# Eight pieces in one operation in the first FFN group, and matmul operands moved to multiples of 512 bytes

## The chip, the core and the metric

The kernel runs on one core of one Trainium2 chip. The metric is the device time of one execution in microseconds (us). The kernel before takes 2956.35 us, the median of three runs from 2955.74 to 2959.2 us.

## The reference

One layer of a streaming encoder is computed for 64 new frames of a running stream ("sample"), 16 meta tokens and 2048 frames of a new stream ("prompt"): 2128 rows of width 1024. The rows go through a projection into three head groups (differential attention, RG-LRU, gated linear attention), an output projection, and an FFN with a causal convolution of width 3 along the rows, separately for the two streams:

```
hn = rms_norm(x, prm['norm_ffn_g'][l])
u = hn @ prm['ffn_w_up'][l]
uc, ffn_c1 = causal_dwconv(u, ffn_c0, prm['ffn_conv_w'][l], prm['ffn_conv_b'][l])
x = x + (jax.nn.gelu(uc) * (hn @ prm['ffn_w_gate'][l])) @ prm['ffn_w_down'][l]
```

The FFN width is 2816. The convolution needs the two rows before each row: zeros ahead of the prompt's first row, two rows of state ahead of the sample's first.

## The kernel before, in words

Activations lie transposed: features on the 128 partitions, rows along the free dimension. Every product is taken with three matmuls of split operands (high by high, high by low, low by high), whose elements have 4 bytes. A weight tile of 128 by 1024 (`whi`, `wlo`, three buffers each) holds eight slices of 128 columns; each matmul loads one slice as its weights and streams a second operand of up to 512 columns past it.

The work of TensorE (PE) is one long stream, `dense`: the input projection (`win`, matmuls at L641 and L643), then the FFN three times, for the row groups `FGROUPS = [[512], [512], [336, 256, 512]]`. Attention (`ps_sc`, `ps_pt`, `ps_o`) and the recurrences are woven into the first part of it by a scheduler that sets each engine's order when the program is built; the third group runs alone. Within a group `wout` (L1434) makes the output projection, its norm fills `h2h`/`h2l`, `up_gate` makes for each of 22 tiles of 128 FFN features the products `pu` and `pg` (L1299) and their activation into `gh`/`gl`, and `down` (L1366) multiplies four such tiles at a time with the down weights into `pd`.

In `up_gate` of the first group the 512 rows are two pieces, the 64 sample rows ("s") and 448 rows of the prompt ("z"). For each piece every step is issued by itself: ACT copies `pu` behind two columns of history in `uh` (L1316) and makes the first tap `cc` (L1321), DVE adds two taps (L1323), ACT squares (L1326), DVE (L1327), ACT takes tanh (L1329); after `pg` two DVE operations (L1334, L1336), POOL rounds into `gh` (L154) and DVE takes the rest `gl` (L157). `uh` and `cc` have two buffers each (`ev2`), so the two pieces of one feature tile fill both.

Where the tiles lie, as the built program has it (bytes within a partition): `whi` begins at 16928, `wlo` at 29216, 32 bytes past a multiple of 512, and so do all their slices. `h2h` and `gh` of the first two groups begin at 41504 and 90656, 32 past a multiple too, with slices 2048 bytes apart. In the third group `h2h`/`h2l` of the 256 and 512 rows are 480 bytes past a multiple (`h2h` of the 512 rows at 196576), and its `gh`/`gl`, 1104 columns long, lie 4416 bytes apart, so that their parts begin at many distances from one. The 256-column operands of `win` are 32 past. The order of allocation gives these places; no engine waits on them.

Of the kernel before, what the change touches and what calls it, by code (L numbers as in the profile page):

```python
# [135 lines left out]
def tile_hymba_step(ctx, tc, xT, xkT, cache_v, wi, wo, wu, wg, wd, par, sgla, c_msk, yT_p, yT_s, nkT_p, nv_p, lh_p, lc_p, gs_p, fc_p,  # L136
# [1138 lines left out]

    def up_gate(g, ff, H, gt, norms):
        (wu_,), (wg_,) = w_take(("up", g, ff), 1), w_take(("gate", g, ff), 1)
        ev2, gp = env["ev"], env["gp"]
        gw = sum(FGROUPS[g])
# [5 lines left out]
        goff = 0  # L1285
        for bi, n in enumerate(FGROUPS[g]):
            yield from norms.pop(bi, ())
            us = []
            for a, b, kind in ffn_pieces(g, n):
                uh = ev2.tile([P, n + 2], F32, tag="uh", name="uh")  # L1290
                cc = ev2.tile([P, n], F32, tag="cc", name="cc")
                us.append((a, b, kind, uh, cc))
# [38 lines left out]
            pg = env["prod"]
            for a, b, kind, uh, cc in us:
                m = b - a
                nc.vector.scalar_tensor_tensor(out=cc[:, :m], in0=cc[:, :m], scalar=0.5, in1=pg[:, a:b], op0=ALU.mult,  # L1334
                                               op1=ALU.mult)
                nc.vector.scalar_tensor_tensor(out=cc[:, :m], in0=uh[:, :m], scalar=1.0, in1=cc[:, :m], op0=ALU.add,  # L1336
                                               op1=ALU.mult)
                gh_, gl_ = gh[:, goff + a:goff + b], gl[:, goff + a:goff + b]
                pool_scaled(gh_, cc[:, :m])
# [295 lines left out]
```

## Time and profile before

| | before |
|---|---|
| median of three runs | 2956.35 us |
| profiled execution | 2957.12 us, span 2955.3 us (1.8 us lie around the span) |
| PE busy | 2841.2 us, 96% of the span |
| DVE, ACT, POOL busy | 1890.9, 1138.1, 870.5 us |
| mean granted TensorE clock | 0.98 of full speed |
| input projection | 0 to 817 us |
| FFN group 1, 2, 3 | 817 to 1487, to 2022, to 2955.3 us |

Times in the text are microseconds from the span's start. A matmul's own duration in the profile includes its way through the array and overlaps its neighbours; what a matmul costs in a dense run is the distance from its start to the next start. The stages are told apart by where `wout` (L1434) begins.

### The profile page before, as it was taken

To read this page: it belongs to the slowest core of one execution; us is meant where nothing else is said; L and a number is where in the kernel's file an instruction comes from. 1 tells how busy PE (TensorE), PEld (TensorE's weight loads), DVE (VectorE), ACT (ScalarE), POOL (GpSimd) and SP (SyncE) were. 2 spreads that over 40 slices of the span, in tenths; PEclk is the share of its full clock that TensorE was granted. 3 is DMA by queue.
4 is the path that set the end of the run, shared out by engine and by line. 5 is a ranking of instruction groups with operands and counts; after the bars stand their busy time and mean duration, and the time that the engine had idled before them with its cause. 6 is when DMAs were issued, how large, how long until landed. Compare 5 with 4: busy or idle time off the path is not lost.

```text
span 2955.3 us, 44538 instructions
## 1 busy us (share of the span) xinstructions
PE 2841.2 (96%) x16031; PEld 2508.7 (85%) x16031; DVE 1890.9 (64%) x3699; ACT 1138.1 (39%) x2589; POOL 870.5 (29%) x1212
## 2 busy tenths in 40 slices
PE   7999999999898998999999999999999999999997
PEld 7988899989876887787787888888989998999997
DVE  7677685778879879879969865333454333333335
ACT  5354554555555454545445433211222121212122
POOL 4435534434535445444424221000110000000001
PEclk9999999999999999999999999999999999999999
DMA  7675564656796776777875565685222222222222
GB/s 241 201 217 148 179 214 139 199 179 186 227 338 212 252 264 234 249 266 261 285 258 183 197 203 183 208 327 186 72 86 86 86 86 86 86 86 86 86 86 105
DMA packets 277930, 537.43 MB, mean 182 GB/s; under 512 B 31014, under 2 KB 170030, under 8 KB 277710
## 3 DMA queue, kind: packets, MB, share of 16 engines
q1 hardware_dynamic: 277566, 534.58, 54.9%
q8 instruction: 127, 2.08, 0.3%
q14 instruction: 93, 0.76, 0.1%
q10 hardware_dynamic: 144, 0.01, 0.0%
HBM read 382.74 MB, written 151.76 MB: 181 GB/s over the span
## 4 chain that ended last, share of the span: by engine, by line
PE 69%; DVE 14%; DMA 4%; issue 2%; ACT 2%; POOL 1%; SPq 0%; POOLq 0%; ACTq 0%; DVEq 0%
PE pd L1366 15%; PE pg L1299 14%; PE pu L1299 14%; PE pd L1434 6%; PE ps_w L641 5%; PE ps_w L643 3%; DVE pc L1100 3%; PE ps_o L1166 3%; PE ps_sc L1059 2%; PE ps_pt L1151 2%; PE ps_sc L1052 2%; DVE BD L886 1%; DVE NB L1061 1%; PE ps_r L891 1%; DVE y L435 1%
## 5 line engine op out<-in xcount | busy, mean ns | idle before, releaser
L257 POOL TENSOR_TENSOR wlo<-raw,whi 128x1024 fp32r<-128x1024 f32 (+1 forms) x104 | 249.8, 2404 | 309.6 <-ACT whi L151 278.5
L1062 ACT ACTIVATE pc<-ps_sc,NB 128x512 f32<-128x512 f32 (+6 forms) x400 | 224.5, 562 | 298.2 <-DVE NB L1061 262.6
L1299 PE MATMUL pu<-h2h,whi 128*128 128x512 f32 (+2 forms) x880 | 316.8, 360 | 5.0 <-ACT h2h L151 2.8
L1323 DVE SCALAR_TENSOR_TENSOR cc<-uh,prm,cc 128x512 f32<-128x512 f32 (+4 forms) x264 | 165.0, 634 | 242.9 <-ACT cc L1321 239.8
L1299 PE MATMUL pu<-h2l,whi 128*128 128x512 f32 (+2 forms) x880 | 316.2, 359 | 1.4 <-DVE h2l L157 1.4
L1299 PE MATMUL pu<-h2h,wlo 128*128 128x512 f32 (+2 forms) x880 | 316.5, 360 | 0.0
L1366 PE MATMUL pd<-gh,whi 128*128 128x512 f32 (+2 forms) x880 | 314.2, 360 | 2.1 <-DMA whi<-WS 1.4
L1299 PE MATMUL pg<-h2h,wlo 128*128 128x512 f32 (+2 forms) x880 | 315.6, 359 | 0.4 <-DMA wlo<-WS 0.4
L1299 PE MATMUL pg<-h2l,whi 128*128 128x512 f32 (+2 forms) x880 | 315.9, 359 | 0.0
L1299 PE MATMUL pg<-h2h,whi 128*128 128x512 f32 (+2 forms) x880 | 315.0, 358 | 0.7 <-DMA whi<-WS 0.5
L1366 PE MATMUL pd<-gh,wlo 128*128 128x512 f32 (+2 forms) x880 | 314.5, 358 | 0.0
L1366 PE MATMUL pd<-gl,whi 128*128 128x512 f32 (+2 forms) x880 | 312.9, 357 | 0.0
L1372 DVE TENSOR_TENSOR x<-x,pd 128x512 f32<-128x512 f32 (+2 forms) x240 | 141.8, 595 | 217.1 <-PE pd L1366 216.1
L641 PE MATMUL ps_w<-hh,whi 128*128 128x384 f32 (+2 forms) x768 | 259.1, 340 | 16.0 <-ACT whi L151 10.5
L1316 ACT ACTIVATE uh<-pu 128x336 f32<-128x336 f32 (+3 forms) x132 | 59.3, 464 | 539.6 <-PE pu L1299 539.1
L1061 DVE TENSOR_REDUCE NB<-ps_sc 128x1 f32<-128x512 f32 (+6 forms) x400 | 209.5, 529 | 86.8 <-PE ps_sc L1059 85.2
L641 PE MATMUL ps_w<-hl,whi 128*128 128x384 f32 (+2 forms) x768 | 259.6, 339 | 0.4 <-DVE hl L157 0.4
L641 PE MATMUL ps_w<-hh,wlo 128*128 128x384 f32 (+2 forms) x768 | 256.0, 335 | 0.3 <-DVE wlo L157 0.3
L154 POOL TENSOR_SCALAR gh<-cc 128x336 fp32r<-128x336 f32 (+3 forms) x132 | 72.9, 553 | 444.8 <-DVE cc L1336 440.0
L151 ACT ACTIVATE whi<-raw 128x1024 fp32r<-128x1024 f32 (+2 forms) x160 | 165.8, 1036 | 96.7 <-DMA raw<-in_wi 30.5
L1299 PEld LDWEIGHTS pu<-h2h,whi 128*128 128x128 f32 x880 | 167.4, 190 | 26.6 <-ACT h2h L151 3.2
L154 POOL TENSOR_SCALAR pc<-pc,fr 128x512 f32<-128x512 f32 (+4 forms) x200 | 156.8, 802 | 109.3 <-DVE fr L1082 86.1
(330 smaller groups left out, 7142.5 us busy)
## 6 DMA issues: line engine op xcount, KB each, us to landing
whi<-WS SPq DMA_DIRECT2D x148, 512.0 KB, 4.3
wlo<-WS SPq DMA_DIRECT2D x148, 512.0 KB, 4.3
raw<-in_wi SPq DMA_DIRECT2D x74, 512.0 KB, 4.1
WS<-whi SPq DMA_DIRECT2D x74, 512.0 KB, 3.1
WS<-wlo SPq DMA_DIRECT2D x74, 512.0 KB, 6.0
Kc<-KHL SPq DMA_DIRECT2D x48, 512.0 KB, 5.8
V<-VHL SPq DMA_DIRECT2D x48, 512.0 KB, 3.5
Q<-QHL SPq DMA_DIRECT2D x64, 256.0 KB, 4.4
```

The source lines that it names most:

```text
L151: nc.scalar.activation(out=out, in_=in_, func=AF.Copy, scale=scale)
L154: nc.gpsimd.tensor_scalar(out, in_, s, 1.0, ALU.mult, ALU.mult)
L257: nc.gpsimd.tensor_tensor(out=lo[:, :n], in0=t[:, :n], in1=f(hi[:, :n]), op=ALU.subtract)
L641: nc.tensor.matmul(ps[:, :n], lhsT=wx, rhs=hx, start=st_, stop=sp_)
L643: nc.tensor.matmul(ps[:n, :wd_], lhsT=hx, rhs=wx, start=st_, stop=sp_)
L1061: nc.vector.tensor_reduce(NB[:qw, ti, m, ci:ci + 1], ps[:qw, :kt_], AX.X, ALU.min)
L1062: nc.scalar.activation(out=pv_[m][:qw, :kt_], in_=ps[:qw, :kt_], func=AF.Exp, scale=-1.0, bias=NB[:qw, ti, m, ci:ci + 1], accum_out=SS[:qw ...
L1299: nc.tensor.matmul(ps[:, :n], lhsT=w_[wi_][:, k * P:(k + 1) * P], rhs=hx, start=(k == 0 and i3 == 0), stop=(k == KT - 1 and i3 == 2))
L1323: nc.vector.scalar_tensor_tensor(out=cc[:, :m], in0=uh[:, w:w + m], scalar=cw[w], in1=cc[:, :m], op0=ALU.mult, op1=ALU.add)
L1366: nc.tensor.matmul(ps[:, :n], lhsT=w_, rhs=g_[:, o:o + n], start=(j == 0 and i3 == 0), stop=(j == len(gts) - 1 and i3 == 2))
L1372: nc.vector.tensor_tensor(x2[b, ct], x2[b, ct], ps[:, :n], ALU.add)
L1434: nc.tensor.matmul(ps[:, :n], lhsT=w_, rhs=g_, start=(k == 0 and i3 == 0), stop=(k == KT - 1 and i3 == 2))
```

## The change

In the first group the 512 rows of a feature tile are now eight pieces of 64 columns. `uh` has room for eight times 66 columns, and each step is issued once over all eight: the copy of `pu` writes 8 by 64 columns, a small ACT operation fills the two history columns of pieces 2 to 7 from the end of the piece before (read from `pu`), and POOL fills those of piece 0 (state) and piece 1 (zeros) as it did. `uh` and `cc` are one tile each per feature tile now, in the same two buffers. The other groups take the same code with one piece.

A tile of 480 bytes, set once by POOL, stands ahead of the weights; a second of 480 bytes ahead of the third group's right-hand pools and a third of 64 bytes ahead of its `gh`. In the third group `gh`/`gl` hold the 512 rows first, then 336 (in room for 384), then 256. In the built program `whi` now begins at 17408, `h2h` of the first two groups at 41984, `gh` at 91136, `h2h` of the third group's 512 rows at 196096 and its `gh` at 83456 with 4608 bytes between tiles, all multiples of 512. (The slices of the 336 rows' `h2h` are 1344 bytes apart, so only the first of them lies on one.)

```
+    nc.gpsimd.memset(cst.tile([P, 120], F32, name="pad0"), 0.0)
...
+        pad(p2.enter_context(tc.tile_pool(name="pad_r", bufs=1, side="right")), 480)
...
+        pad(p2.enter_context(tc.tile_pool(name="pad_l", bufs=1)), 64)
...
-            for a, b, kind, uh, cc in us:
-                m = b - a
...
-                nc.scalar.activation(out=uh[:, 2:2 + m], in_=pu[:, a:b], func=AF.Copy)
...
-                nc.scalar.activation(out=cc[:, :m], in_=uh[:, 0:m], func=AF.Identity, scale=cw[0], bias=cb)
...
+            pu = env["prod"][:, :n].rearrange("p (c t) -> p c t", t=t)
+            nc.scalar.activation(out=uh[:, :, 2:], in_=pu, func=AF.Copy)
+            if g == 0:
+
+                nc.gpsimd.tensor_copy(uh[:, 0, 0:2], pr("fst", 0, 44).rearrange("p (w k) -> p k w", w=2)[:, ff, :])
+                nc.gpsimd.memset(uh[:, 1, 0:2], 0.0)
+                nc.scalar.activation(out=uh[:, 2:, 0:2], in_=pu[:, 1:n // t - 1, t - 2:], func=AF.Copy)
+                nc.gpsimd.tensor_copy(fce[:, 1, :, ff], uh[:, 0, t:])
...
+            nc.scalar.activation(out=cc, in_=uh[:, :, 0:t], func=AF.Identity, scale=cw[0], bias=cb)
+            for w in (1, 2):
+                nc.vector.scalar_tensor_tensor(out=cc, in0=uh[:, :, w:w + t], scalar=cw[w], in1=cc, op0=ALU.mult,
+                                               op1=ALU.add)
...
+    def places(g):
+
+        at, n = {}, 0
+        for b in sorted(range(len(FGROUPS[g])), key=lambda b: -FGROUPS[g][b]):
+            at[b] = n
+            n += -(-FGROUPS[g][b] // P) * P
+        return at, n
+
+    def pad(pool, n):
+        nc.gpsimd.memset(pool.tile([P, n // 4], F32, tag="pad", name="pad", bufs=1), 0.0)
```

ACT's order around one feature tile of the first group, before (`whi<-raw` splits weights, `pc,SS<-ps_sc` is attention's exponential, `ph<-ps_pt` rounds its weights):

```order
L1316 ACTIVATE uh<-pu 128x64
L1316 ACTIVATE uh<-pu 128x448
L1321 ACTIVATE cc<-uh,prm 128x64
L1062 ACTIVATE pc,SS<-ps_sc,NB 128x16
L151 ACTIVATE ph<-ps_pt 128x512
```

```order
L1321 ACTIVATE cc<-uh,prm 128x448
L1326 ACTIVATE uh<-cc 128x64
L1329 ACTIVATE uh<-uh 128x64
L1326 ACTIVATE uh<-cc 128x448
L1329 ACTIVATE uh<-uh 128x448
```

Between the two stands one more row of attention; the second piece follows the first at each step. The same feature tile now:

```order
L1312 ACTIVATE uh<-pu 128x8x64
L1317 ACTIVATE uh<-pu 128x6x2
L1322 ACTIVATE cc<-uh,prm 128x512
L1063 ACTIVATE pc,SS<-ps_sc,NB 128x16
L151 ACTIVATE ph<-ps_pt 128x512
```

```order
L1328 ACTIVATE uh<-cc 128x8x64
L1330 ACTIVATE uh<-uh 128x8x64
L151 ACTIVATE whi<-raw 128x1024
L1063 ACTIVATE pc,SS<-ps_sc,NB 128x144 x2
L151 ACTIVATE oo<-oSs 128x256
```

Eight operations of the convolution became five, and the attention rows between them kept their places. On DVE, a place a little later in the first group, before (`att`, `EK`, `BD` are the gated linear attention, `pl` is attention's):

```order
L1327 SCALAR_TENSOR_TENSOR uh<-uh,cc 128x64
L1323 SCALAR_TENSOR_TENSOR cc<-uh,prm,cc 128x448
L895 COPY_PREDICATED att<-msk,ps_r 128x64x4
L157 TENSOR_TENSOR pl<-ps_pt,ph 16x256
L1327 SCALAR_TENSOR_TENSOR uh<-uh,cc 128x448
L1334 SCALAR_TENSOR_TENSOR cc<-cc,pg 128x64
L1334 SCALAR_TENSOR_TENSOR cc<-cc,pg 128x448
L1336 SCALAR_TENSOR_TENSOR cc<-uh,cc 128x64
L1336 SCALAR_TENSOR_TENSOR cc<-uh,cc 128x448
```

and the same steps now:

```order
L1329 SCALAR_TENSOR_TENSOR uh<-uh,cc 128x8x64
L896 COPY_PREDICATED att<-msk,ps_r 128x64x4
L879 TENSOR_TENSOR EK<-bl 128x128
L880 TENSOR_TENSOR EK<-bl 128x128
L157 TENSOR_TENSOR pl<-ps_pt,ph 16x256
L1333 SCALAR_TENSOR_TENSOR cc<-cc,pg 128x512
L1334 SCALAR_TENSOR_TENSOR cc<-uh,cc 128x512
```

The 64-column operations are gone and two rows of the recurrence moved in among the rest. On PE no matmul is added or removed; in the first group attention's matmuls stand a few places earlier or later among those of the FFN, and ahead of it and in the third group the order is the same.

## Rows read from the trace of the kernel before

**Rows 1.** The page: busy time and share of the span of each engine, and the chain that ended last by engine.

```profile
PE 2841.2 (96%) x16031; PEld 2508.7 (85%) x16031; DVE 1890.9 (64%) x3699; ACT 1138.1 (39%) x2589; POOL 870.5 (29%) x1212
...
PE 69%; DVE 14%; DMA 4%; issue 2%; ACT 2%; POOL 1%; SPq 0%; POOLq 0%; ACTq 0%; DVEq 0%
```

**Rows 2.** Busy time of each engine by stage (input projection, FFN groups 1, 2 and 3), then the mean granted clock, the DMA engines' busy share and GB/s.

```profile
0.00:817.00 817.00, 763.40 (x4928) 719.50 (x4929) 611.35 (x1287) 414.76 (x1022) 358.29 (x403) 0.97 0.65 195
817.00:1487.00 670.00, 635.66 (x3120) 521.13 (x3119) 577.76 (x1128) 348.69 (x808) 306.19 (x384) 0.97 0.77 260
1487.00:2022.00 535.00, 528.57 (x2581) 438.98 (x2580) 321.57 (x587) 182.79 (x407) 113.76 (x192) 0.99 0.66 225
2022.00:2955.30 933.30, 913.59 (x5407) 829.08 (x5405) 380.19 (x700) 191.89 (x356) 92.21 (x233) 0.99 0.25 90
```

**Rows 3.** Group 1 (817 to 1487): whom PE and ACT waited for, total us, times, longest us; then the chain by line in the same stretch.

```profile
PE ps_sc L1052 <- ACT pc L1062: 16.3, 15, 3.5
...
ACT pc L1062 <- DVE NB L1061: 112.4, 66, 8.1
...
ACT cc L1321 <- DVE gl L157: 9.8, 3, 5.9
```

```profile
by line: PE pd L1366 11.6%; PE pu L1299 7.4%; DVE pc L1100 7.1%; PE pg L1299 6.8%; PE pd L1434 6.6%; issue 5.1%; PE ps_o L1166 4.2%; DVE BD L886 3.4%; DVE NB L1061 3.4%; DVE cc L1323 3.2%; PE ps_sc L1059 2.9%; PE ps_sc L1052 2.9%; PE ps_pt 
```

**Rows 4.** The convolution's DVE operations in group 1 by shape: count, busy us and mean ns of one, idle before.

```profile
L1323 DVE SCALAR_TENSOR_TENSOR cc<-uh,prm,cc 128x448 f32<-128x448 f32 x44 | 33.8, 768 | 1.4 <-ACT cc L1321 1.2
L1323 DVE SCALAR_TENSOR_TENSOR cc<-uh,prm,cc 128x64 f32<-128x64 f32 x44 | 20.6, 468 | 6.2 <-ACT cc L1321 6.0
L1336 DVE SCALAR_TENSOR_TENSOR cc<-uh,cc 128x448 f32<-128x448 f32 x22 | 15.7, 714 | 0.2
L1327 DVE SCALAR_TENSOR_TENSOR uh<-uh,cc 128x448 f32<-128x448 f32 x22 | 15.1, 688 | 2.2 <-ACT uh L1326 2.1
L157 DVE TENSOR_TENSOR gl<-cc,gh 128x448 fp32r<-128x448 f32 x22 | 13.6, 618 | 2.2 <-POOL uh L1313 1.7 <-POOL gh L154 0.2
L1334 DVE SCALAR_TENSOR_TENSOR cc<-cc,pg 128x448 f32<-128x448 f32 x22 | 13.5, 612 | 0.0
L1336 DVE SCALAR_TENSOR_TENSOR cc<-uh,cc 128x64 f32<-128x64 f32 x22 | 10.7, 488 | 0.1
L157 DVE TENSOR_TENSOR gl<-cc,gh 128x64 fp32r<-128x64 f32 x22 | 5.6, 253 | 0.3
L1327 DVE SCALAR_TENSOR_TENSOR uh<-uh,cc 128x64 f32<-128x64 f32 x22 | 4.7, 214 | 0.7 <-ACT uh L1326 0.7
L1334 DVE SCALAR_TENSOR_TENSOR cc<-cc,pg 128x64 f32<-128x64 f32 x22 | 4.7, 212 | 0.5 <-PE pg L1299 0.3
```

**Rows 5.** The same operations with 512 columns, over the whole span.

```profile
L1323 DVE SCALAR_TENSOR_TENSOR cc<-uh,prm,cc 128x512 f32<-128x512 f32 x88 | 66.6, 758 | 148.2 <-ACT cc L1321 146.9
...
L1336 DVE SCALAR_TENSOR_TENSOR cc<-uh,cc 128x512 f32<-128x512 f32 x44 | 30.8, 699 | 3.4
...
L157 DVE TENSOR_TENSOR gl<-cc,gh 128x512 fp32r<-128x512 f32 x44 | 30.4, 692 | 27.1 <-POOL gh L154 26.4 <-POOL r L414 0.7
L1327 DVE SCALAR_TENSOR_TENSOR uh<-uh,cc 128x512 f32<-128x512 f32 x44 | 30.4, 691 | 26.6 <-ACT uh L1326 26.4
L1334 DVE SCALAR_TENSOR_TENSOR cc<-cc,pg 128x512 f32<-128x512 f32 x44 | 30.2, 686 | 33.3 <-PE pg L1299 33.1
```

**Rows 6.** A run of 512-column matmuls of group 2 without a break, weights and streamed operand 32 bytes past a multiple of 512: first and 49th start (start us, duration us).

```profile
1905.10 0.39 PE L1299 MATMUL pu<-h2h,wlo 128*128 128x512 f32 x1
...
1915.98 0.39 PE L1299 MATMUL pu<-h2h,wlo 128*128 128x512 f32 x1
```

**Rows 7.** The same in group 3, streamed operand 480 past: 512 columns, first and 48th; 256 columns, first and 48th.

```profile
2414.32 0.40 PE L1299 MATMUL pu<-h2h,whi 128*128 128x512 f32 x1
...
2425.29 0.40 PE L1299 MATMUL pg<-h2h,wlo 128*128 128x512 f32 x1
```

```profile
2408.67 0.28 PE L1299 MATMUL pu<-h2h,whi 128*128 128x256 f32 x1
...
2414.20 0.28 PE L1299 MATMUL pg<-h2h,wlo 128*128 128x256 f32 x1
```

**Rows 8.** `down` of group 3, one run of 512 columns, first and 12th; and 256-column matmuls of the input projection, both operands 32 past, first and 27th.

```profile
2331.32 0.39 PE L1366 MATMUL pd<-gh,whi 128*128 128x512 f32 x1
...
2333.85 0.39 PE L1366 MATMUL pd<-gl,whi 128*128 128x512 f32 x1
```

```profile
397.21 0.28 PE L643 MATMUL ps_w<-whi,hl 128*128 128x256 f32 x1
...
400.31 0.28 PE L643 MATMUL ps_w<-whi,hh 128*128 128x256 f32 x1
```

**Rows 9.** The two runs' stretches: busy PE, PEld, DVE, ACT, POOL, then clock, DMA share, GB/s.

```profile
1905.00:1916.00 11.00, 11.00 (x51) 9.10 (x50) 3.59 (x6) 2.68 (x4) 1.26 (x5) 1.00 0.95 346
2414.30:2425.50 11.20, 11.20 (x50) 9.06 (x49) 3.90 (x7) 3.18 (x6) 0.72 (x3) 1.00 0.25 94
```

**Rows 10.** From the page, matmuls by line over the span (each of L1299 in six such rows, L1366 and L641 in three).

```profile
L1299 PE MATMUL pu<-h2h,whi 128*128 128x512 f32 (+2 forms) x880 | 316.8, 360 | 5.0 <-ACT h2h L151 2.8
...
L1366 PE MATMUL pd<-gh,whi 128*128 128x512 f32 (+2 forms) x880 | 314.2, 360 | 2.1 <-DMA whi<-WS 1.4
...
L641 PE MATMUL ps_w<-hh,whi 128*128 128x384 f32 (+2 forms) x768 | 259.1, 340 | 16.0 <-ACT whi L151 10.5
```

**Rows 11.** What POOL's pacing copies of group 3's loads (L1392) waited for, total us and times; and a fill of 128 columns at the start.

```profile
  PE pg L1299: 8.8, 2
```

```profile
0.87 0.20 POOL L295 MEMSET ones<- 128x128 f32 x1
...
14.97 2.71 POOL L257 TENSOR_TENSOR wlo<-raw,whi 128x1024 fp32r<-128x1024 f32 x1 [13.21 <-ACT whi L151]
```

More of the change, by code (lines that the diff above doesn't have):

```diff
@@ L1278, in up_gate @@
         ev2, gp = env["ev"], env["gp"]
-        gw = sum(FGROUPS[g])
+        at, gw = places(g)
         gh = gp.tile([P, gw], F32R, tag="gh", name="gh")
@@ L1284, in up_gate @@
         cb = pr("fcb", ff)
-        goff = 0
         for bi, n in enumerate(FGROUPS[g]):
+            goff = at[bi]
             yield from norms.pop(bi, ())
[L1288 to L1292, printed above, removed]
+            uh, cc = taps(g, n)
+            t = n if g else NS
             def product(w_):
@@ L1330, in up_gate @@
-            yield from product(wg_)
[L1331 to L1339, printed above, removed]
-                minus(gl_, cc[:, :m], f(gh_))
@@ L1341, in up_gate @@
-            goff += n
-        w_used(2)
+            pu = env["prod"][:, :n].rearrange("p (c t) -> p c t", t=t)
[5 more added lines that the diff above has]
+                nc.gpsimd.tensor_copy(fce[:, 1, :, ff], uh[:, 0, t:])
+            else:
+                nc.gpsimd.tensor_copy(uh[:, 0, 0:2], halo[:, ff, :])
@@ new lines, in up_gate @@
+            nc.gpsimd.tensor_copy(halo[:, ff, :], uh[:, uh.shape[1] - 1, t:])
+            nc.scalar.activation(out=cc, in_=uh[:, :, 0:t], func=AF.Identity, scale=cw[0], bias=cb)
+            for w in (1, 2):
+                nc.vector.scalar_tensor_tensor(out=cc, in0=uh[:, :, w:w + t], scalar=cw[w], in1=cc, op0=ALU.mult,
+                                               op1=ALU.add)
+            uh = uh[:, :, 0:t]
+            nc.scalar.activation(out=uh, in_=cc, func=AF.Square, scale=GELU_A)
+            nc.vector.scalar_tensor_tensor(out=uh, in0=uh, scalar=1.0, in1=cc, op0=ALU.add, op1=ALU.mult)
@@ new lines, in up_gate @@
+            nc.scalar.activation(out=uh, in_=uh, func=AF.Tanh, scale=GELU_B)
+            yield from product(wg_)
+            pg = env["prod"][:, :n].rearrange("p (c t) -> p c t", t=t)
+            nc.vector.scalar_tensor_tensor(out=cc, in0=cc, scalar=0.5, in1=pg, op0=ALU.mult, op1=ALU.mult)
+            nc.vector.scalar_tensor_tensor(out=cc, in0=uh, scalar=1.0, in1=cc, op0=ALU.add, op1=ALU.mult)
+            gh_, gl_ = gh[:, goff:goff + n], gl[:, goff:goff + n]
+            cc = cc.rearrange("p c t -> p (c t)")
@@ L1344, in offsets @@
+            pool_scaled(gh_, cc)
+            minus(gl_, cc, f(gh_))
+        w_used(2)
+    def places(g):
[6 more added lines that the diff above has]
+        nc.gpsimd.memset(pool.tile([P, n // 4], F32, tag="pad", name="pad", bufs=1), 0.0)
     def offsets(g):
@@ L1359, in down @@
                 W[half] = w_take(("down", g, q, half), len(gts) // 2)
-            o, n = offsets(g)[b], FGROUPS[g][b]
+            o, n = places(g)[0][b], FGROUPS[g][b]
             ps = env["ps"].tile([P, NMAX], F32, tag="w", name="pd")
```

29 lines of the change are left out of this document (7 added, 22 removed).

## The prediction

> **What bounds the kernel now.** I read the busy times and the chain first, then the stages, then the waits of the stage that the convolution's edit touches, and last the distance from one matmul's start to the next. The reader is to see in the first that PE is busy for 2841.2 of 2955.3 us and that the chain runs through PE for 69% and DVE for 14% [rows 1]: what shortens matmuls anywhere shortens the kernel, and what relieves another engine counts only where PE waits for it. By stage, PE is idle for 670 - 635.7 = 34.3 us in FFN group 1, for 6.4 in group 2 and for 19.7 in group 3; in group 1 DVE is busy for 577.8 of 670 us, 86%, and the clock averages 0.97 of full speed, 2.4 GHz, because it falls to 1.2 GHz for stretches in that stage [rows 2]. PE's largest wait there is 16.3 us for attention's exponential, and ACT itself waited 112.4 us for the row minimum (`NB`) that DVE makes [rows 3]. So group 1 has two limits close together, PE and DVE; groups 2 and 3 have PE alone.
>
> The last view is the one on which the second half of the change rests. In group 2, 48 distances between 512-column matmuls take 1915.98 - 1905.10 = 10.88 us, 226.7 ns each [rows 6]. In group 3, 47 take 10.97 us, 233.4 ns, and 47 of 256 columns take 5.53 us, 117.7 ns [rows 7]. The same instruction on the same clock costs 6.7 ns more in group 3. It isn't the DMA: the faster stretch ran beside a DMA share of 0.95, the slower beside 0.25, and the other engines were about as busy [rows 9]. What differs is the place of the streamed operand: as far past a multiple of 512 bytes as the weights (32 and 32), or not (480 and 32).
>
> **The convolution.** Per feature tile the edit removes six 64-column DVE operations (L1323 twice, and L1327, L1334, L1336, L157) and widens six from 448 to 512 columns. The 64-column ones take 20.6 + 10.7 + 5.6 + 4.7 + 4.7 = 46.3 us in all, the 448-column ones 33.8 + 15.7 + 15.1 + 13.6 + 13.5 = 91.7 [rows 4]. With 512 columns, by the means of the other groups, a tile takes 2 x 0.758 + 0.699 + 0.691 + 0.686 + 0.692 = 4.28 us, 22 tiles 94.3 [rows 5]. DVE's work falls by 46.3 + 91.7 - 94.3 = 43.7 us, 8% of what it does in that stage. ACT and POOL lose their 64-column operations too; ACT gains one operation of 12 columns. `uh` and `cc`, of which the two pieces of one feature tile filled both buffers, now hold two feature tiles; the 9.8 us for which ACT stood at `cc` for the tile before to be done [rows 3] should go.
>
> How much of that reaches the end: the chain in group 1 names L1323 for 3.2% of 670 us, 21.4 us [rows 3]; of that line's 54.4 us the 64-column part is 20.6, so about 8 us of chain go. The other four lines are too small to be named in the chain; for them and for ACT's wait I add half as much, 4. I take -12. The bounds: nothing, if DVE's gain is spent waiting for POOL and ACT at other places; -34.3, if all of PE's idle time in the stage goes. On the other side, no row shows a DVE operation over eight pieces with gaps between them. At its dearest each piece would cost what a 64-column operation costs now, 214 ns for L1327: six operations of 1.71 us on 22 tiles are 226 us for 138 now, +88, DVE would be busy for all of the stage, and at the chain's rate (21.4 us on the chain for 54.4 busy) that is +35. I stay with the plain 512-column row, the nearest in columns and in kind.
>
> **The places of the operands.** Afterwards weights and streamed operands both begin at a multiple of 512 in all three groups and in the input projection. Their distance from each other was zero already in groups 1 and 2; only group 3's changes. I take a matmul of group 3 to cost then what the same shape costs where the two lie alike. For 512 columns: `up_gate` has 22 x 48 = 1056 in group 3 and `wout` 8 x 24 = 192, so 1248 x 6.7 ns = 8.4 us. `down` has 22 x 8 x 3 = 528; a run of it takes 2.53 us for 11 distances, 230.0 ns [rows 8], so 528 x 3.3 = 1.7 us. For 256 columns it goes against: where both lie 32 past, 26 distances take 3.10 us, 119.2 ns [rows 8], 1.5 ns more than group 3's 117.7; 1776 x 1.5 = 2.7 us. The 336-column ones are left as they are, three quarters of their `h2h` slices lying elsewhere than on a multiple anyway. The term is -8.4 - 1.7 + 2.7 = -7.4, taken as -7. Its bounds come with the rivals, as the trace has no stretch with both operands on a multiple.
>
> A rule of the skill speaks against this term. The rows give 226.7 and 233.4 ns for one shape [rows 6, 7]. The Trainium skill, "TensorE: Matmul & The Clock Gate", section "Step-by-step: what each phase is for", has it that the streamed operand and the weights come through two independent read ports, so that loading the next weights takes nothing from the running matmul; by that, places would not matter, the term would be nothing and the sum 2945. The trace does not agree, unless something unseen sets the two groups apart.
>
> **What costs nothing.** The three fills: the first, 120 columns at the start, stands where POOL idles for 13.21 us ahead of its next operation, and a fill of 128 columns takes 0.20 us [rows 11]. The second waits for what attention leaves on the right side, as the first pacing copy did; such copies waited 8.8 us for PE in all [rows 11], and behind it on POOL stand two halo copies and the loads of group 3, of which PE in group 2, busy for 528.57 of 535 us [rows 2], doesn't wait. Without that cover such a wait, 8.8 us at most by this row, would stand at the start of group 3.
>
> **The sum.** 2957.12 (the profiled execution) - 12 - 7 = 2938. That execution is 0.8 us over the median of the three runs, which differ by 3.5 among themselves, so I leave it at 2938.
>
> **The rivals.**
>
> *Every matmul gets shorter.* A dense 512-column matmul costs 226.7 ns, of which 512 columns at 2.4 GHz are 213.3; 13.4 ns are extra at the best place that the trace has [rows 6]. If what costs them is that an operand begins in the middle of something, they shrink everywhere and not in group 3 alone. Lines 1299, 1366 and 641 have 6 x 880, 3 x 880 and 3 x 768 matmuls [rows 10], 10,224 in all; half the extra on each, 6.7 ns, is 68.5 us: 2938 - 68 = 2870. All of it would be 2801, and some more from L643 and `wout`. For it: the extra is about as large for 256 columns (117.7 against 106.7). Against it: nothing in the trace shows a smaller extra, and 256 columns are no better at 32 and 32 than elsewhere. The Trainium skill, in the same page's section "Back-to-back issue gap", gives N / 2.4 + 2.5 ns for this distance, 215.8 for 512 columns; by it nearly all of the extra could go, but no row here comes near it.
>
> *Places don't matter.* Group 3 stays at 233.4 for a reason not seen, and the convolution's 12 remain: 2945.
>
> *On a multiple is the worse place.* The two streams then begin at the same point of whatever 512 bytes repeat, in all groups. If 512 columns cost in groups 1 and 2 what group 3 pays today, 2 x 1776 x 6.7 = 23.8 us are added and group 3 gains nothing: 2957 + 24 - 12 = 2969, slower. For it: 256 columns are dearer at 32 and 32 than at 480 and 32. It decides once group 2's distance passes 226.7 + 12 / 3.552 = 230.1 ns.
>
> *The convolution's gain is hidden.* DVE's saved time turns into waits, and only group 3's 7 remain: 2950.
>
> **How the numbers follow.** The forecast has a chance of 0.38, every matmul shorter 0.25, places don't matter 0.12, the worse place 0.13, the gain hidden 0.12. A measurement of this kernel can tell about 0.2%, 6 us, from no change. Below 2950.4 lie nearly all of the first (0.36), the second, and most of the third (0.09) and half of the last less a little (0.04): faster 0.74. Within 6 us: 0.02, 0.03 and 0.07, and 0.02 of the fourth: 0.14. Slower: the rest of the fourth and 0.01 of the last: 0.12. The range reaches down over most of the second case, to 2860, and up to 2962, which leaves the fourth out. The likeliest case's own range is 2925 to 2950.
>
> **What would show it.** In the profile after: 512-column matmuls of group 3 start 226.7 ns apart, and those of group 2 as before (both near 220 or below: the first rival; both at 230 or more: the worse place; 233.4 and 226.7: places don't matter). The 8 by 64-column DVE operations take about 0.69 to 0.76 us; DVE is busy some 40 us less in group 1; PE's idle time there falls from 34 to about 22; ACT no longer waits for `gl` at `cc`. It is wrong if group 1 shortens by less than 5 us, or if a stage without any edit of order, the input projection, changes its length by more than 3.

## The result, and the profile after

| | before | after |
|---|---|---|
| median, four runs each | 2957.77 us | 2927.98 us |
| lowest to highest | 2955.74 to 2960.65 | 2925.70 to 2931.39 |
| ratio | | 0.990, 95% interval 0.9882 to 0.9917 |
| profiled execution | 2957.12, span 2955.3 | 2931.39, span 2929.6 |

The changed kernel is 29.8 us faster by the medians, 25.7 by the two profiled executions. The page of the changed kernel, busy times, as the first line of [rows 1]:

```profile
PE 2826.5 (96%) x16031; PEld 2503.0 (85%) x16031; DVE 1874.0 (64%) x3567; ACT 1125.3 (38%) x2523; POOL 861.6 (29%) x1193
```

PE's 14.7 us less is over half of the 25.7; the rest is time in which it no longer stands. The stages, with the columns of [rows 2]:

```profile
0.00:819.40 819.40, 767.05 (x4930) 723.58 (x4931) 610.39 (x1288) 415.05 (x1022) 358.83 (x404) 0.97 0.64 194
819.40:1465.20 645.80, 622.99 (x3123) 509.94 (x3121) 564.14 (x995) 337.17 (x743) 298.88 (x361) 0.99 0.81 269
1465.20:1999.80 534.60, 527.93 (x2579) 437.49 (x2578) 319.81 (x587) 181.45 (x404) 111.81 (x194) 0.99 0.65 225
1999.80:2929.60 929.80, 908.49 (x5405) 831.97 (x5403) 379.65 (x700) 191.66 (x356) 92.11 (x234) 0.99 0.26 90
```

Against [rows 2] the input projection is 2.4 us longer, group 1 is 24.2 shorter, group 2 0.4, group 3 3.5 shorter. In group 1 PE's idle time went from 34.3 to 645.8 - 622.99 = 22.8 us, and the clock from 0.97 to 0.99 of full speed: summed from the trace's granted clock, PE spent 41.0 us of that stage at 1.2 GHz before and 10.2 after. A microsecond at 1.2 GHz does about half a microsecond's work (512-column matmuls start 427 ns apart there, 227 at 2.4 GHz), so that is some 15.4 us, beside 11.5 of idle time; together 26.9, which is 2.7 more than the stage shortened by.

The waits of group 1, to be read beside [rows 3]:

```profile
ACT pc L1063 <- DVE NB L1062: 112.0, 62, 8.1
```

```profile
PE ps_sc L1053 <- ACT pc L1063: 6.7, 8, 2.9
```

PE's wait for attention's exponential fell from 16.3 to 6.7 us; ACT's wait for the row minimum stayed; ACT's wait for `gl` at `cc` is gone. The convolution on DVE in group 1, the shapes after that answer to [rows 4]:

```profile
L1324 DVE SCALAR_TENSOR_TENSOR cc<-uh,prm,cc 128x512 f32<-128x512 f32 x44 | 42.4, 963 | 1.8 <-ACT cc L1322 1.6
...
L1334 DVE SCALAR_TENSOR_TENSOR cc<-uh,cc 128x512 f32<-128x512 f32 x22 | 20.5, 930 | 1.1 <-ACT uh L1330 0.4
L157 DVE TENSOR_TENSOR gl<-cc,gh 128x512 fp32r<-128x512 f32 x22 | 16.8, 763 | 2.2 <-POOL gh L154 2.1
L1329 DVE SCALAR_TENSOR_TENSOR uh<-uh,cc 128x512 f32<-128x512 f32 x22 | 15.3, 694 | 4.8 <-ACT uh L1328 4.8
L1333 DVE SCALAR_TENSOR_TENSOR cc<-cc,pg 128x512 f32<-128x512 f32 x22 | 14.9, 679 | 0.9 <-PE pg L1303 0.5
```

That is 109.9 us where it was 138.0, 28 less and not 44: the two taps and the last product take 963 and 930 ns on average, not the 758 and 699 of [rows 5]. A few long ones make the difference. The taps of the stage (shortest, median and longest in ns), and one of the long ones beside the operation in which POOL splits a weight tile into `wlo`:

```profile
L1324 DVE SCALAR_TENSOR_TENSOR cc<-uh,prm,cc x44: 729/746/2880, 931.2 to 1420.0; 128x512 f32<-128x512 f32 x44
...
1038.05 2.74 POOL L258 TENSOR_TENSOR wlo<-raw,whi 128x1024 fp32r<-128x1024 f32 x1
...
1038.46 2.88 DVE L1324 SCALAR_TENSOR_TENSOR cc<-uh,prm,cc 128x512 f32<-128x512 f32 x1
```

This tap ends at 1041.34, 0.55 us after POOL's split. Of the 132 operations of the convolution, fourteen lie over 150 ns above the median of their shape, 17.0 us in all, and thirteen of these overlap such a split. Eleven of them began while one was running. All eleven have their operands in SBUF, the memory in which the tiles lie, and all ended 546 to 551 ns after the split; only one more, which began 7 ns after a split did, took its usual time. The product that reads `pg` from PSUM, where matmuls leave their sums (L1333), took its usual 677 ns inside a split. Before, 22.6 of the 138.0 us were such excess: the 468 ns of a 64-column tap in [rows 4] are a mean that eight long ones make, and the median is 278. Summed by medians the work fell from 115.6 to 92.9 us. No run takes POOL's splits away, so this is read from the times and not tried. DVE's busy time in the stage fell by 577.76 - 564.14 = 13.6 us only: its other operations there took 14.5 more.

Group 3, a run of 512 columns (first and 48th start) and one of 256 (likewise), as [rows 7]:

```profile
2150.09 0.40 PE L1303 MATMUL pu<-h2h,whi 128*128 128x512 f32 x1
...
2160.77 0.39 PE L1303 MATMUL pg<-h2h,wlo 128*128 128x512 f32 x1
...
2168.41 0.28 PE L1303 MATMUL pu<-h2h,whi 128*128 128x256 f32 x1
...
2174.04 0.28 PE L1303 MATMUL pg<-h2h,wlo 128*128 128x256 f32 x1
```

47 distances in 10.68 us are 227 ns for 512 columns (233.4 before), 47 in 5.63 are 119.8 for 256 (117.7 before). Over all of `up_gate` and `wout` in the stage the means are 227.3 and 119.8. Groups 1 and 2 have 227 to 229 on average, as before.

### The profile page after: what moved, and what is told of

It reads as the page before. It is cut to its first block, busy times and chain, and to the rows that moved or that the text cites. A ratio compares the mean times of both kernels' runs of the same rounds, so it can differ in the third digit from the quotient of the medians.

```text
span 2929.6 us, 44244 instructions
## 1 busy us (share of the span) xinstructions
PE 2826.5 (96%) x16031; PEld 2503.0 (85%) x16031; DVE 1874.0 (64%) x3567; ACT 1125.3 (38%) x2523; POOL 861.6 (29%) x1193
## 4 chain that ended last, share of the span: by engine, by line
PE 74%; DVE 12%; DMA 7%; issue 3%; ACT 2%; POOL 1%; SPq 1%; POOLq 0%; ACTq 0%; DVEq 0%
PE pu L1303 15%; PE pg L1303 15%; PE pd L1374 15%; PE ps_w L642 6%; PE pd L1442 5%; PE ps_w L644 4%; PE ps_o L1167 3%; PE ps_sc L1060 2%; PE ps_sc L1053 2%; PE ps_pt L1152 2%; DMA Q<-QHL 2%; PE ps_r L892 1%; DVE pc L1101 1%; DVE NB L1062 1%; DMA raw<-in_wi 1%
## 5 line engine op out<-in xcount | busy, mean ns | idle before, releaser
L1324 DVE SCALAR_TENSOR_TENSOR cc<-uh,prm,cc 128x512 f32<-128x512 f32 (+2 forms) x220 | 156.0, 709 | 235.8 <-ACT cc L1322 232.9
L1312 ACT ACTIVATE uh<-pu 128x512 f32<-128x512 f32 (+2 forms) x110 | 57.6, 524 | 527.0 <-PE pu L1303 523.9
L154 POOL TENSOR_SCALAR gh<-cc 128x512 fp32r<-128x512 f32 (+2 forms) x110 | 63.6, 578 | 465.6 <-DVE cc L1334 456.4
L1374 PEld LDWEIGHTS pd<-gh,whi 128*128 128x128 f32 x880 | 165.6, 188 | 26.3 <-DVE x L1380 4.9
```

The costliest lines, as they stand in the source:

```text
L154: nc.gpsimd.tensor_scalar(out, in_, s, 1.0, ALU.mult, ALU.mult)
L1324: nc.vector.scalar_tensor_tensor(out=cc, in0=uh[:, :, w:w + t], scalar=cw[w], in1=cc, op0=ALU.mult, op1=ALU.add)
L1374: nc.tensor.matmul(ps[:, :n], lhsT=w_, rhs=g_[:, o:o + n], start=(j == 0 and i3 == 0), stop=(j == len(gts) - 1 and i3 == 2))
```

## The experiments

Theory 1: two independent gains, the convolution's in group 1 and the operands' distance in group 3. Within the first, theory W (DVE's saved work) stands against theory B (two feature tiles in flight), and theory C adds the clock that follows PE's idle gaps.

### Each half of the change by itself

The convolution alone (`places` as running offsets, fills left out):

```
-    nc.gpsimd.memset(cst.tile([P, 120], F32, name="pad0"), 0.0)
...
-        pad(p2.enter_context(tc.tile_pool(name="pad_r", bufs=1, side="right")), 480)
...
-        pad(p2.enter_context(tc.tile_pool(name="pad_l", bufs=1)), 64)
...
-        for b in sorted(range(len(FGROUPS[g])), key=lambda b: -FGROUPS[g][b]):
+        for b in range(len(FGROUPS[g])):
...
-            n += -(-FGROUPS[g][b] // P) * P
+            n += FGROUPS[g][b]
```

> The convolution's edit alone: weights and streamed operands lie as in the kernel before, and PE, DVE and ACT take their work in the order of the changed kernel. Theory 1 (two independent gains: group 1 gains by the convolution, group 3 by the distance between weights and streamed operand): about 2931, that is 2957 less the 24 us that group 1 lost; group 3 keeps its 933 us and its 233 ns for a 512-column matmul. Rival A (the places do most of it, in group 1 too): 2945 or later, and group 1 stays above 660 us. Rival B (places matter nowhere, group 3's 3.5 us come from the order of work): 2928, the same as the changed kernel, and group 3 at 930.

The places alone are the three fills and `places` added to the kernel before:

> The places of the operands alone: fills and places as in the changed kernel, convolution in two pieces, and the order of work of the kernel before. Theory 1: group 3 shortens by 3 to 4 us (512-column matmuls from 233.4 to 227 ns, 256-column ones from 117.7 to 120), groups 1 and 2 and the input projection keep their lengths; 2953 to 2954. Rival A: group 1 shortens by 10 or more. Rival B: no stage changes, 2957.

Measured: the convolution alone 0.9933 of before (0.9920 to 0.9946), the places alone 0.9989 (0.9979 to 1.0000); of 2951 us that is 20 and 3 us. Groups 1 and 3 of the first, then of the second:

```profile
816.00:1461.30 645.30, 626.04 (x3123) 513.50 (x3121) 564.59 (x995) 337.05 (x743) 299.20 (x361) 0.99 0.81 270
...
1997.10:2932.10 935.00, 914.61 (x5405) 829.26 (x5403) 379.61 (x700) 191.60 (x356) 92.58 (x233) 0.99 0.25 90
```

```profile
809.10:1483.40 674.30, 639.10 (x3118) 523.42 (x3117) 581.16 (x1127) 348.67 (x807) 304.98 (x384) 0.96 0.77 258
...
2019.60:2949.40 929.80, 910.02 (x5405) 833.40 (x5403) 379.75 (x700) 191.58 (x356) 92.79 (x234) 0.99 0.25 90
```

Theory 1 holds by the stages: the first has group 1's gain and group 3's old length, the second the reverse (its group 1 is 4 us longer than before, with 51 us at 1.2 GHz for 41). PE, DVE and ACT take their work in the same order in the first as in the changed kernel, and in the second as in the kernel before, so the 3 to 5 us of group 3 are the places, and none of group 1's 24 is. The two ratios multiply to 0.9922, 23 us, where the whole change measured 0.990 and, in a second run further down, 0.9908, 27 to 30. With intervals of 0.001 to 0.002 on either side that is no contradiction, but no chip ran all three, and where the rest lies isn't shown.

### Distance or multiple

The changed kernel with a fill of 64 bytes ahead of the pools of groups 1 and 2:

```
+        pad(env["hs"].enter_context(tc.tile_pool(name="pad_h", bufs=1)), 64)
         env["hp"] = env["hs"].enter_context(tc.tile_pool(name="hp2", bufs=1))
```

> The changed kernel with 64 bytes put ahead of the streamed operands of groups 1 and 2, so that they lie 64 bytes past a multiple of 512 and the weights on one; group 3 as in the changed kernel. If the distance between weights and streamed operand counts: 512-column matmuls of groups 1 and 2 go from 227 to about 233 ns, group 2 grows by (1056 + 192) x 6.5 + 528 x 2.5 ns = 9.4 us, group 1 by up to as much; 2940 to 2950. If group 3's 233 ns had another reason: nothing changes, 2928.

Measured: 2930.66 us, 0.9936 of before. Its group 2, and 512 columns there (first and 48th start):

```profile
1462.70:1999.90 537.20, 530.08 (x2579) 437.84 (x2578) 320.43 (x587) 182.13 (x405) 113.01 (x194) 0.99 0.65 224
```

```profile
1879.88 0.39 PE L1304 MATMUL pu<-h2h,whi 128*128 128x512 f32 x1
...
1890.63 0.39 PE L1304 MATMUL pg<-h2h,wlo 128*128 128x512 f32 x1
```

10.75 us for 47 distances are 228.7 ns: dearer than at distance 0, but by 2 ns and not by the 6 of group 3 before, and group 2 grew by 2.6 us and not by 9.4. I had taken the price at 64 bytes on one side for that at 64 on the other; both theories as I put them missed. The distances one by one, with nothing of the kernel left in: no projection, attention or FFN, only runs of 24 matmuls.

```
+    def run(name, n, d, wo_, reps):
...
+            c = r % 8 * P + wo_
+            nc.tensor.matmul(ps[:, :n], lhsT=w[:, c:c + P], rhs=M[:, d:d + n], start=(r == 0), stop=(r == reps - 1))
```

> No part of the computation is left in; only runs of 24 matmuls, the weights of each from another 128 columns, the streamed operand at 0 to 512 bytes from the weights' phase, for 512, 384, 336, 256 and 128 columns, each twice; and three with the weights 32 bytes off. If the distance counts: 512 columns cost 226 to 228 ns at 0 and 512 and about 233 at 64 and 448; 256 columns 119 to 120 at 0 and 117.7 at 448; the weights at 32 bytes and the streamed operand at 32 cost what both at 0 cost. If the multiple itself counts: weights and streamed operand both at 32 are dearer or cheaper than both at 0. If neither: one figure for each width.

First start of a run and of the next; the names carry the columns and the streamed operand's distance in elements of 4 bytes, and those with a w have the weights 32 bytes past:

```profile
54.20 0.39 PE L177 MATMUL at512x0x<-m,wa 128*128 128x512 f32 x1
59.64 0.40 PE L177 MATMUL at512x1x<-m,wa 128*128 128x512 f32 x1
...
82.07 0.39 PE L177 MATMUL at512x16x<-m,wa 128*128 128x512 f32 x1
87.56 0.40 PE L177 MATMUL at512x24x<-m,wa 128*128 128x512 f32 x1
...
148.99 0.40 PE L177 MATMUL at512x112x<-m,wa 128*128 128x512 f32 x1
154.59 0.40 PE L177 MATMUL at512x120x<-m,wa 128*128 128x512 f32 x1
...
165.66 0.39 PE L177 MATMUL wat512x0x<-m,wa 128*128 128x512 f32 x1
171.26 0.40 PE L177 MATMUL wat512x8x<-m,wa 128*128 128x512 f32 x1
176.70 0.40 PE L177 MATMUL wat512x16x<-m,wa 128*128 128x512 f32 x1
...
374.84 0.28 PE L177 MATMUL at256x8x<-m,wa 128*128 128x256 f32 x1
377.65 0.28 PE L177 MATMUL at256x16x<-m,wa 128*128 128x256 f32 x1
...
853.94 0.28 PE L177 MATMUL at256x0x<-m,wa 128*128 128x256 f32 x1
856.81 0.28 PE L177 MATMUL wat256x0x<-m,wa 128*128 128x256 f32 x1
```

24 matmuls of 512 columns take 5.44 us at distance 0 (226.7 ns), 5.49 at 64 bytes (228.8), 5.60 at 448 (233.3). With the weights at 32 a streamed operand at 0 costs 233.3 (5.60), one at 32 226.7 (5.44): for 512 columns the distance counts, the multiple doesn't. 24 of 256 columns take 2.87 us at 0 and 2.81 at 32. The first few distances of a run still vary; over the second half of each run, in ns, both passes alike but where two figures stand:

| bytes apart | 512 columns | 256 columns | 336 columns |
|---|---|---|---|
| 0, 256, 512 | 226.7 | 120.0 | 153.3 |
| 32, 288 | 233.3 | 116.7, 117.8 | 153.3 |
| 64, 320 | 228.9 | 117.8 | 153.3 |
| 192, 448 | 233.3 | 113.3, 117.8 | 155.8 |
| 4 | 236.7 | 123.3 | 156.7 |

It repeats every 256 bytes, and the best place for 512 columns is the worst of these for 256 but one. Where 256 columns have two figures, the distance alone doesn't decide: 32 cost 116.7 in both passes with the weights on a multiple and 117.8 with them 32 past one. Why the distance matters no run shows.

### DVE's work or two tiles in flight

The kernel before with buffers of their own for the 64-column piece:

```
-                uh = ev2.tile([P, n + 2], F32, tag="uh", name="uh")
-                cc = ev2.tile([P, n], F32, tag="cc", name="cc")
+                m = NS if kind == "s" else n
+                uh = ev2.tile([P, m + 2], F32, tag="uhs" if kind == "s" else "uh", name="uh")
+                cc = ev2.tile([P, m], F32, tag="ccs" if kind == "s" else "cc", name="cc")
```

> The kernel before with buffers of their own for the 64-column piece, so that uh and cc of two feature tiles are in flight, and not one operation of the convolution less. Theory W (group 1 gained 24 us because DVE has less to do: fewer idle gaps of PE, and with fewer gaps less time at the 1.2 GHz clock): group 1 stays at 665 to 672 us, with 32 to 36 us of PE idle and 40 to 50 us at 1.2 GHz; 2956 on the first chip's scale, the same as before. Theory B (the gain is that two feature tiles are in flight): ACT's wait at cc goes and group 1 falls to 645 to 652.

The changed kernel with one buffer in group 1:

```
-        uh = env["ev"].tile([P, max(wide, n + 2)], F32, tag="uh", name="uh")
-        cc = env["ev"].tile([P, n], F32, tag="cc", name="cc")
+        uh = env["ev"].tile([P, max(wide, n + 2)], F32, tag="uh" if g else "uhs", name="uh", bufs=2 if g else 1)
+        cc = env["ev"].tile([P, n], F32, tag="cc" if g else "ccs", name="cc", bufs=2 if g else 1)
```

> The changed kernel with one buffer each for uh and cc in group 1: the work is saved, but one feature tile at a time is in flight, as before. Theory W: group 1 stays at 645 to 652 us although ACT waits at cc again. Theory B: group 1 goes back to 662 or more.

The changed kernel with six 64-column operations per feature tile put back, and then with three of them:

```
+                again(g, uh[:, 0, w:w + NS], cw[w], cc[:, 0, :NS], ALU.mult, ALU.add)
...
+    def again(g, a, s, b, op0, op1):
+        if g == 0:
+            nc.vector.scalar_tensor_tensor(out=scr[:, :NS], in0=a, scalar=s, in1=b, op0=op0, op1=op1)
```

> The changed kernel with six DVE operations of 64 columns put back per feature tile of group 1 at the places where the kernel before had them, their results into a tile that nothing reads: some 40 to 46 us of DVE work in 132 operations, buffers and ACT as in the changed kernel. Theory W: group 1 goes back to 660 to 670 us, PE idle 30 to 35, and the time at 1.2 GHz to 30 to 45 us. Theory B: 645 to 650, with 22 us idle and about 10 at 1.2 GHz. Half of it (655) would say that the work and the rest share the gain.

> As the run with six small DVE operations put back, with three of the six: both at the convolution's taps and the one at the last residue, 66 operations in all. Theory W, DVE's work counts in proportion: half of what six cost, 10 to 18 us over the changed kernel. Rival (a threshold: what matters is that DVE's share passes a point): below 5 us, or nearly the whole 30.

> The changed kernel as it is, beside the next two on one chip, as their scale: 0.990 of before, and a second profile, which tells by how much stage lengths and the time at 1.2 GHz differ from one execution to another; 3 to 5 us of length and 10 us of half clock are expected.

Groups 1 and 2 of the kernel with six put back:

```profile
810.20:1495.60 685.40, 648.38 (x3197) 528.08 (x3196) 603.43 (x1151) 342.76 (x767) 300.75 (x365) 0.98 0.78 257
1495.60:2027.40 531.80, 521.16 (x2505) 428.68 (x2504) 312.85 (x562) 171.51 (x380) 111.19 (x190) 0.99 0.65 222
```

It has 74 matmuls more in group 1 than the changed kernel and 74 fewer in group 2 (3197 and 2505 for 3123 and 2579): attention work moved, as it did by 40 with one tile in flight and by 9 the other way with two tiles and no work saved. So groups 1 and 2 are compared together, DVE's busy time and PE's idle time from such rows, the time at 1.2 GHz from the granted clock; us. Each ratio is against the kernel before on the same chip; the other columns come from one execution each, which can lie 8 us from its kernel's median (2934.24 for 2942.25 with one tile in flight):

| | ratio to before (95%) | groups 1+2 | DVE busy | PE idle | at 1.2 GHz |
|---|---|---|---|---|---|
| before | | 1205.0 | 899.3 | 40.8 | 51.2 |
| places alone | 0.9989 (0.9979, 1.0000) | 1210.5 | 903.1 | 39.8 | 68.3 |
| two tiles in flight, no work saved | 0.9997 (0.9981, 1.0014) | 1196.7 | 891.9 | 39.3 | 27.3 |
| work saved, one tile in flight | 0.9962 (0.9944, 0.9980) | 1194.6 | 888.8 | 32.7 | 41.0 |
| both (convolution alone) | 0.9933 (0.9920, 0.9946) | 1181.1 | 884.9 | 27.2 | 20.5 |
| changed kernel again | 0.9908 (0.9889, 0.9926) | 1182.4 | 884.7 | 29.4 | 18.9 |
| three operations put back | 0.9947 (0.9931, 0.9963) | 1193.8 | 893.1 | 35.1 | 37.5 |
| six put back | 1.0024 (1.0013, 1.0036) | 1217.2 | 916.3 | 47.7 | 47.8 |

Neither W nor B stands alone. Two tiles in flight without less work bring nothing that the whole time shows, though ACT's wait at `cc` is gone. Groups 1 and 2 were 8 us shorter in that execution and group 3, which the edit doesn't touch, 3 longer; the other 5 are no gain, as the kernel before itself has a median of 2953.32 on that chip and 2957.77 on the first. With the places' 3 us taken off, the saved work brings 8 us with one tile in flight and 20 to 27 with two. With DVE's work put back while the buffers stay, everything goes: 12 us for three operations (2940.94 against 2928.87 on one chip), about 34 for six (ratio 1.0024 against 0.9908). Three cost a third of what six do, inside the 10 to 18 us of theory W, and the threshold falls. ACT's and POOL's saved operations were never put back, so their own part of the gain isn't tested. What the six cost on DVE in group 1:

```profile
L1349 DVE SCALAR_TENSOR_TENSOR scr<-uh,cc 128x64 f32<-128x64 f32 x44 | 16.1, 365 | 0.6
L1349 DVE SCALAR_TENSOR_TENSOR scr<-uh,prm,cc 128x64 f32<-128x64 f32 x44 | 15.3, 347 | 0.5
L1349 DVE SCALAR_TENSOR_TENSOR scr<-cc,gh 128x64 f32<-128x64 f32 x22 | 5.2, 238 | 0.0
L1349 DVE SCALAR_TENSOR_TENSOR scr<-cc,pg 128x64 f32<-128x64 f32 x22 | 4.7, 215 | 0.2
```

These 41.3 us come on top of the 512-column operations, which take 16 more in this kernel than the 448-column ones did; DVE ends 17 us busier in groups 1 and 2 than before, and the kernel is slower than before.

The columns of length, idle time and clock close the account: groups 1 and 2, less PE's idle time and half of the time at 1.2 GHz, are 1138.6 us before, 1143.5 in the changed kernel's second run and 1136.5 to 1145.6 in all eight. The whole gain is idle time and clock; the matmuls of the two groups didn't get cheaper.

### What brings the clock down

Before, around 1325, PE stood for 2.3 us; the stretch ahead, the gap, what followed, and after it (columns as in [rows 2]):

```profile
1320.00:1325.10 5.10, 5.10 (x25) 3.92 (x22) 5.10 (x4) 0.58 (x1) 4.97 (x4) 1.00 0.60 147
1325.10:1327.70 2.60, 0.27 (x2) 0.23 (x2) 2.60 (x8) 1.06 (x4) 0.00 (x0) 1.00 1.03 364
1327.70:1334.50 6.80, 6.80 (x18) 4.47 (x18) 6.21 (x14) 5.60 (x14) 1.99 (x6) 0.50 0.85 302
1334.50:1340.00 5.50, 5.50 (x25) 4.54 (x25) 4.71 (x11) 4.92 (x12) 1.28 (x1) 1.00 0.83 314
```

Group 1 before has eight gaps of 1.9 us or more (2.0 to 4.4), all but one with such a stretch behind them; after, it has two (2.9 and 2.4). To see whether the gap is the cause, the changed kernel got gaps in group 3, where PE hardly waits (one execution):

```
+    LONG = {3: 2, 6: 4, 9: 8, 12: 2, 15: 4, 18: 8}
...
+                if (g, bi) == (2, 2) and w_ is wg_ and ff in LONG:
+                    for _ in range(LONG[ff]):
+                        nc.vector.tensor_copy(scr, env["prod"])
+                    nc.vector.tensor_copy(ps[:, 0:1], scr[:, 0:1])
```

> The changed kernel with six idle gaps of PE made in group 3, in feature tiles 3, 6, 9, 12, 15 and 18: ahead of one product VectorE copies the product before it to scratch 2, 4, 8, 2, 4 and 8 times (about 0.7 us each) and then writes one column into the bank of the next, for which PE has to wait. Theory C (PE's idle gaps bring the clock down, and that is the part of the 24 us which I did not price): the gaps of about 3 and 6 us are followed by 3 to 7 us each at 1.2 GHz, and group 3 grows by the sum of the gaps (about 20 us) and half of that time, 6 to 14 us more. Rival (the time at 1.2 GHz in group 1 has nothing to do with gaps): the clock stays at 2.4 GHz behind them and group 3 grows by the gaps alone.

```profile
2408.30:2414.30 6.00, 6.00 (x33) 5.22 (x31) 2.23 (x4) 1.42 (x2) 0.19 (x1) 1.00 0.34 128
2414.30:2417.90 3.60, 0.00 (x1) 0.00 (x0) 3.56 (x6) 1.20 (x2) 0.00 (x0) 1.00 0.20 77
2417.90:2424.70 6.80, 5.01 (x12) 4.02 (x13) 1.54 (x3) 0.06 (x1) 0.00 (x0) 0.50 0.00 0
2424.70:2430.70 6.00, 6.00 (x35) 5.48 (x34) 2.25 (x4) 1.12 (x2) 1.26 (x3) 1.00 0.36 123
...
2664.50:2667.10 2.60, 0.62 (x3) 0.55 (x4) 2.45 (x5) 0.71 (x2) 0.00 (x0) 1.00 0.30 123
2667.10:2670.50 3.40, 3.40 (x10) 2.66 (x9) 0.00 (x0) 0.55 (x1) 0.00 (x0) 0.50 0.02 5
```

Only two of the six became gaps, 5.4 us at 2414 and 2.0 at 2664; at the other places PE didn't wait for the column. Both were followed by half clock, 6.8 and 3.4 us, at places where the kernel without them runs at 2.4 GHz. Group 3 is 942.8 us long for 929.8: 7.4 of gaps and 5.1 of half clock make 12.5 of the 13.0. Theory C holds at these two gaps, and the rival falls there. The Trainium skill, "TensorE: Matmul & The Clock Gate", section "Part 1: The HAM clock gate (the "warmup" mystery)", has the slow clock as the idle state that activity releases; these rows agree, with 6.8 and 3.4 us at 1.2 GHz behind the gaps and 2.4 GHz after them. A long gap isn't all that can stand ahead of it: in group 2 of the changed kernel the clock fell for 3.4 us at 1539.0 and again at 1549.2, where PE's longest idle time shortly before was 0.75 and 0.43 us, among attention's short matmuls. What brought it down there is open.

### A better version

By the table of distances the 256-column operands are better 32 bytes from the weights' phase, while 512 columns stay at 0:

```
+            if tg[:2] == "h2" and n == 256:
+                a = pool.tile([P, KT * n + P], F32R, tag=f"{tg}{bi}", name=f"{tg}{bi}", bufs=1)
+                return a[:, 8:8 + KT * n].rearrange("p (k n) -> p k n", k=KT)
...
-            at[b] = n
+            at[b] = n + (8 if FGROUPS[g][b] == 256 else 0)
...
+            n += P if at[b] % P else 0
```

> The changed kernel with the streamed operands of 256 columns in group 3 put 32 bytes past a multiple of 512, the weights on one; the order of work on all engines is that of the changed kernel. By the runs of single distances 256 columns cost 119.8 ns at distance 0 and 116.7 at 32: 1776 x 3.1 = 5.5 us, group 3 from 929.7 to about 924, the other stages as they are; 0.9905 of before where the changed kernel has 0.9925 on the same scale. If in the kernel another thing sets the 256-column matmuls' distance: 120 ns and 930 us as in the changed kernel.

Its group 3, and 256 columns there, first and 48th start:

```profile
1988.90:2913.70 924.80, 904.91 (x5405) 827.73 (x5404) 379.64 (x700) 191.83 (x356) 92.29 (x234) 0.99 0.26 91
```

```profile
2156.65 0.28 PE L1307 MATMUL pu<-h2h,whi 128*128 128x256 f32 x1
...
2162.14 0.28 PE L1307 MATMUL pg<-h2h,wlo 128*128 128x256 f32 x1
```

5.49 us for 47 distances, 116.8 ns; group 3 is 5.0 us shorter than in the changed kernel, where 5.5 were expected. 2919.38 us, 0.9882 of before (0.9860 to 0.9904). Against the changed kernel the whole time can't decide, as the intervals overlap; group 3's length and the 116.8 ns show the gain. With attention's weights (Q) moved to the phase of K as well:

> The changed kernel with the 256-column operands of group 3 at 32 bytes, and the weights of attention's scores (Q) at the phase of the streamed K (they lay 224 bytes apart; 288 past is 32 past by the repeat of 256 bytes that the single distances showed); the order of work on all engines as in the changed kernel. 384 matmuls of 512 columns x 6.6 ns = 2.5 us at most from Q, 5.5 from the 256-column ones: 6 to 8 us below the changed kernel. If the scores wait for DVE and ACT anyway, 5 to 6.

2918.64 us, 0.9874 (0.9849 to 0.9899), 10 us below the changed kernel on the same chip. Group 3 is 925.7 us there. What Q's place adds can't be told from the difference between two executions. Where two 512-column matmuls of the scores follow each other, they start 229.6 ns apart and not 233.0, which on 384 of them is 1.3 us, where 2.5 was the most expected.

## Why the prediction was right, and where its terms were off

The direction and the place were right: 2928 us lies in the likeliest case's range of 2925 to 2950, and both gains come from where they were put. The two terms were off by more than their sum shows, -12 for -24 and -7 for -3.5 in the profiled execution: one too small and one too large, so that the sum comes as near as it does in part by luck.

- **The convolution, -12: too small, the clock was missing.** The step "about 8 us of chain, half as much for the others" gave 12 us, and PE's idle time fell by 11.5, from 34.3 to 22.8 where 22 was forecast. That the figure fits is luck in part: the 20.6 us behind the "8" held 8.5 of excess beside POOL's splits, and the "half as much" had no row. And I counted idle time alone. The prediction's first part reads the 1.2 GHz stretches from [rows 2], and the sum then leaves them out: with the gaps went 31 of 41 us at half clock, 15 us. For the same reason the bound of -34.3, "all of PE's idle time", was no bound.
- **DVE's work, -43.7: measured -28, and DVE's busy time in the stage -13.6 where some 40 were forecast.** The step "with 512 columns, by the means of the other groups" set means with few long operations beside POOL's splits against means of [rows 4] that hold many; in group 1 the taps and the last product came out 27% and 33% dearer. By medians the work fell by 115.6 - 92.9 = 22.7 us. The excess of the long ones didn't go with the small operations. POOL has 46 splits in the stage in both kernels, and over all of DVE's operations there the excess over the medians beside them is 61 us before and 62 after.
- **ACT's wait at `cc`: gone as forecast.** By itself it was worth nothing: it is gone with two tiles in flight and no work saved, and the time stays. With the work saved it was worth more than its share of the 4 us: one tile in flight brings 8.6 us of that wait back and costs 12 to 18.
- **The places, -7: half of it.** 512 columns came near the forecast, from 233.3 to 227.3 ns, 1248 x 6.0 = 7.5 us for 8.4. `down` went from 230.8 to 229.1, 528 x 1.7 = 0.9 us for 1.7. The 256-column term was the miss. The run of [rows 7] cost 117.7, but four of the stage's 26 long runs cost 113.4 and the mean was 117.2; afterwards it is 119.6 and not 119.2, so 1776 x 2.4 = 4.3 us go against, not 2.7. The 336 columns gained 0.4. The sum is -4.5; PE's busy time in group 3 fell by 913.59 - 908.49 = 5.1, and 1.6 us more idle time leave 3.5.
- **The fills: nothing**, as forecast; group 3's idle time has no new wait that names them.
- **The rivals.** Every matmul shorter: false, groups 1 and 2 keep their 227 to 229 ns, and no distance goes below 226.7 for 512 columns. Places don't matter: false by the runs of single distances; 512 columns with the same weight loads cost 226.7 or 233.3 ns by the distance alone. The Trainium skill, "TensorE: Matmul & The Clock Gate", section "Step-by-step: what each phase is for", gives the streamed operand and the weights two independent read ports; that alone doesn't explain these figures. A multiple is the worse place: false, for 512 columns it is as good as 32 and 32. The convolution's gain hidden: false, it was twice the forecast.
- **A sign that was set too tight:** "wrong if the input projection changes by more than 3". It took 805.6 to 819.4 us in kernels that leave its work alone, 17 to 48 us of it at 1.2 GHz.

## What to carry to other kernels

Price a gap of PE with the clock behind it: where the granted clock falls after gaps, a removed gap gives back its own length and half of the slow stretch, here more than double. What decides for long streamed operands is their distance from the weights, modulo 256 bytes here, not a multiple: measure it for each width, since 512 and 256 columns want different places. And take an operation's duration from the stage it will run in, with its median beside its mean: here the long ones ended just after another engine's work, and most of their excess stayed when the operations went.

## What was not expected of the hardware

The distance between weights and streamed operand moves a 512-column matmul from 226.7 to 236.7 ns and a 256-column one from 113.3 to 123.3. At 192 and 448 bytes 256 columns have two figures, 113.3 and 117.8, in the two passes; group 3 of the kernel before, 448 apart, has both too, 113.4 and 117.7. A 512-column DVE operation of the convolution that begins on SBUF operands during POOL's split of a weight tile ends 0.55 us after it, in eleven cases of twelve. And 128 columns, each with a weight load, hardly gain over 256; first starts of two runs of 24 from the runs of single distances:

```profile
450.03 0.27 PE L177 MATMUL at128x40x<-m,wa 128*128 128x128 f32 x1
452.71 0.28 PE L177 MATMUL at128x48x<-m,wa 128*128 128x128 f32 x1
```

2.68 us for 24 are 111.7 ns, at every distance tried (109.3 in the first run of each pass).
